# Two query tiles in one matmul of the values, eight adjoining units for them, and a longer transfer time in the plan of a four-layer kernel

## The chip, the cores and the metric

The kernel runs as one program on one core of a Trainium2 chip. The metric is the device time of one execution in microseconds (us), the median of three runs. PE is TensorE, DVE VectorE, ACT ScalarE, POOL GpSimd; SP issues most DMAs. The profile shows the TensorE clock that was granted in a stretch as a share of its full speed: 1.0 is 2.4 GHz, 0.5 is 1.2 GHz, and what lies between is a mean over time at both.

## The reference

1024 rows of 1024 float32 columns go through two blocks of two layers each. Cut to what matters here:

```
# block 1, two layers: chunked delta rule + gated linear attention
o = concat(delta_heads(x @ w_in), gla_heads(x @ w_in))
x = layer_norm(ALPHA * x + o @ w_out)
# block 2, layer 0: neighbourhood attention, layer 1: grouped attention
h = x * (1 + sc1) + sh1
y = mixer(h) @ w_o
x = layer_norm_2(ALPHA_2 * x + (1 + g1) * y)
y = hierarchical_moe(x * (1 + sc2) + sh2)      # 32 experts, top 2 of one group
x = layer_norm_2(ALPHA_2 * x + (1 + g2) * y)
# grouped attention: 16 query heads, 4 key/value heads of 64 columns
s = einsum('bqkgd,bskd->bkgqs', qb, k) * scale
p = softmax(s)
o = einsum('bkgqs,bskd->bqkgd', p, v)
```

## The kernel before

**Units.** All large data lies in 47 units ("slot", one of 128 x 1024 float32 each) that the class `Arena` hands out; a `User` has a reserve (`peak`) that others of lower rank leave free. PSUM has 8 banks. A unit can be taken as F32 or as F32R, the rounded form that PE reads in one pass. A float32 operand that must be exact is split into a high and a low F32R part (`split`: ACT rounds, DVE subtracts).

**Order.** The program is a set of generators (`Chain`) with a rank each. `Flow` gives every operation a cost and keeps a clock for each engine; the chain that may go on next emits its instructions. The costs decide nothing on the chip but the order in which instructions stand on each engine. A transfer that POOL issues is counted as `late` by the third argument of `spend`: 12 us with a `compute_op`, else 3 us. `Rows.put` adds a finished tile of 128 rows to a buffer in memory by such a transfer, and its unit is given back when the plan says that it has landed:

```
h = yield from K.A.take(user)
F.vector.tensor_mul(h.f, x.f, r.f)
F.gpsimd.dma_start(dst[t * 128:(t + 1) * 128, :], h.f, accum_op=ALU.add)
yield from F.until(F.last(h.f))
K.A.give(h)
```

**Output projections.** `out_proj_ln` runs at the end of each of the four layers' mixers, over 8 tiles of 128 rows. `load` brings a tile of the mixer's output (`oTm` in block 2) and its row of `x` (`xb`), `split` makes a high and a low part, `one` multiplies (48 matmuls of 512 columns a tile), `finish` normalises, turns the tile (8 transposes) for the next layer and calls `put`. `wout` holds 16 F32R units, the turned rows of the next layer another 16, and the mixer's late heads 4. Ahead of the first `put` `Rows.prepare` loads four rows (`ln_g`, `ln_b`, two of `mod`), computes with them, and `preset` writes the start values of the buffers, eight transfers of 512 KB each (to `xb` and to `Y`). In block 2 the last tile is followed by the routing (`route`), after which the experts start; their weights go through SP's queue too (22 units may wait), and stream without a break from then on.

**Grouped attention.** `gqa_tile` makes one tile of 128 queries of one head: 4 matmuls for the scores, maximum, exponential, scale, 8 transposes. `gqa_close` multiplies the turned probabilities of two heads with the values (`Vb`), the two heads in the two halves of PE's columns. `feed`, the projection of the next heads, fills in at a lower rank.

## Time and profile before

| | |
|---|---|
| median of 3 runs | 4102.42 us (4100.18 to 4103.45) |
| profiled execution | 4100.02 us, span 4098.2 us |
| mean granted clock | 0.967 |
| PE busy | 3826.4 us, 93% |
| DVE, ACT, POOL busy | 77%, 54%, 18% |

Nearly all instructions are recorded by one helper and so have the line L72; they are told apart by tile names and shapes. Times in a timeline count from the span's start. The layers lie, in us: hybrid 0 to 612, its projection to 745, hybrid 1 to 1284, its projection to 1435, neighbourhood attention to 1860, projection and routing to 2005, experts to 2605, layer norm to 2650, grouped attention to 3246, projection and routing to 3440, experts to 4047.

### The profile page before, as it was taken

The page shows a single profiled execution, that of the slowest core. Times are in us where ns is not written, and L with a number is a line of the kernel's source. Part 1 is how long each engine was busy: PE and PEld are TensorE (multiplying, and loading weights), DVE is VectorE, ACT ScalarE, POOL GpSimd, SP SyncE. Part 2 cuts the span into 40 slices and gives each one's busy share as a digit, 9 for nine tenths or more (in the row PEclk, how much of TensorE's full clock was granted, in tenths as well). Part 3 has the DMA queues.
Part 4 walks back from the last instruction along what each step waited for, and adds up shares of the span by engine and source line. Part 5 has one row for each costly group of instructions (what it writes and reads, how often), then busy time and mean ns, then how long its engine had stood idle before and what let it go on. Part 6 is the DMA issues. An engine that isn't in the chain of part 4 may idle for free. (4 is left out here: it accounts for less than half of the span.)

```text
span 4098.2 us, 62930 instructions
## 1 busy us (share of the span) xinstructions
PE 3826.4 (93%) x23000; PEld 3123.1 (76%) x23000; DVE 3145.8 (77%) x5986; ACT 2207.1 (54%) x3931; POOL 756.7 (18%) x608
## 2 busy tenths in 40 slices
PE   7999998999999999999799999789999987999996
PEld 6888787788888777777677777687777875777774
DVE  7777775776775687867888899866658766888887
ACT  4333343433333455442477777567778615777773
POOL 2111100211210222321222222320000011222212
PEclk9999999999999999999899999899999997999998
DMA  4223424211123544327899999610001476999993
GB/s 154 75 85 102 146 87 101 48 38 47 50 78 111 130 139 129 114 98 231 280 366 365 368 369 379 173 23 22 22 6 65 146 200 256 359 360 368 366 363 136
DMA packets 347117, 712.56 MB, mean 174 GB/s; under 512 B 60884, under 2 KB 191630, under 8 KB 346804
## 3 DMA queue, kind: packets, MB, share of 16 engines
q1 hardware_dynamic: 320308, 645.99, 44.0%
q0 software_dynamic: 26496, 62.51, 7.4%
q8 instruction: 182, 2.98, 0.3%
q14 instruction: 131, 1.07, 0.1%
HBM read 626.94 MB, written 115.44 MB: 181 GB/s over the span
## 5 line engine op out<-in xcount | busy, mean ns | idle before, releaser
L72 PE MATMUL banks<-slot 128*128 128x512 f32 (+9 forms) x18258 | 3231.3, 343 | 81.9 <-ACT slot L72 55.6
L72 PEld LDWEIGHTS banks<-slot 128*128 128x128 f32 (+5 forms) x18258 | 2547.4, 177 | 625.7 <-issue 96.9
L72 DVE TENSOR_TENSOR slot<-slot 128x1024 fp32r<-128x1024 f32 (+13 forms) x1445 | 1360.0, 964 | 245.1 <-ACT slot L72 168.2
L72 ACT ACTIVATE slot<-slot 128x1024 fp32r<-128x1024 f32 (+5 forms) x1011 | 998.1, 1016 | 630.0 <-DVE slot L72 193.3
L72 ACT ACTIVATE slot<-banks 128x512 f32<-128x512 f32 (+8 forms) x1124 | 552.4, 513 | 673.5 <-PE banks L72 611.1
L72 PE MATMUL banks<-c,slot 128*128 128x128 f32 (+2 forms) x3484 | 510.3, 283 | 93.7 <-DVE slot L72 24.0
L72 PEld LDWEIGHTS banks<-c,slot 128*128 128x128 f32 (+1 forms) x3484 | 426.3, 158 | 195.8 <-issue 53.1
L72 DVE TENSOR_TENSOR slot<-banks,slot 128x512 fp32r<-128x512 f32 (+4 forms) x622 | 360.6, 608 | 91.7 <-ACT slot L72 48.3
L72 POOL TENSOR_TENSOR slot<-slot 128x384 f32<-128x384 f32 (+2 forms) x184 | 225.6, 1251 | 982.3 <-PE banks L72 416.8
L72 ACT ACTIVATE slot<-slot,small 128x1024 f32<-128x1024 f32 (+1 forms) x292 | 266.4, 926 | 184.5 <-DVE small L72 168.1
L72 DVE COPY slot<-banks 128x512 f32<-128x512 f32 (+6 forms) x406 | 220.0, 551 | 101.6 <-PE banks L72 81.1
L72 POOL DMA_INDIRECT Y<-slot,small x62 | 146.0, 2354 | 354.7 <-DVE slot L72 232.4
L72 ACT ACTIVATE slot<-banks,small 128x1024 f32<-128x1024 f32 x140 | 156.9, 1124 | 66.4 <-DVE small L72 65.9
L72 DVE TENSOR_REDUCE small<-banks 128x1 f32<-128x1024 f32 x128 | 154.7, 1221 | 41.7 <-PE banks L72 40.1
L72 PE MATMUL banks<-slot,small 128*128 128x512 f32 (+2 forms) x388 | 156.1, 524 | 23.3 <-ACT small L72 15.0
L72 POOL MEMSET slot<- 128x1024 f32 (+1 forms) x70 | 67.6, 968 | 578.2 <-PE banks L72 371.1
L72 POOL DMA_DIRECT2D xb<-slot x40 | 35.1, 885 | 725.2 <-DVE slot L72 581.3
L72 DVE SCALAR_TENSOR_TENSOR slot<-slot,c_act 128x1024 f32<-128x1024 f32 x84 | 119.7, 1426 | 34.5 <-DMA slot<-in_ada_w 26.2
L72 DVE SCALAR_TENSOR_TENSOR small<-small 128x1 f32<-128x1 f32 (+3 forms) x590 | 120.1, 211 | 11.7
L72 DVE TENSOR_TENSOR slot<-slot,banks 128x512 f32<-128x512 f32 (+4 forms) x110 | 72.7, 666 | 72.5 <-PE banks L72 72.4
L72 PE MATMUL banks<-small,slot 128*128 128x128 f32 (+1 forms) x576 | 105.2, 297 | 21.0 <-DVE small L72 17.6
L72 ACT ACTIVATE small<-banks 128x64 f32<-128x64 f32 (+2 forms) x289 | 78.7, 273 | 76.9 <-PE banks L72 69.6
(131 smaller groups left out, 1811.6 us busy)
## 6 DMA issues: line engine op xcount, KB each, us to landing
slot<-in_moe_w_up SPq DMA_DIRECT2D x260, 512.0 KB
slot<-in_moe_w_gate SPq DMA_DIRECT2D x260, 512.0 KB
slot<-in_moe_w_down SPq DMA_DIRECT2D x260, 512.0 KB
slot<-in_ada_w SPq DMA_DIRECT2D x96, 512.0 KB
slot<-in_w_in SPq DMA_DIRECT2D x56, 512.0 KB
xb<-slot SPq DMA_DIRECT2D x40, 512.0 KB
xb<-slot POOLq DMA_DIRECT2D x40, 512.0 KB, 5.6
slot<-xb SPq DMA_DIRECT2D x24, 512.0 KB
```

The source lines that it names most:

```text
L72: r = real(*a, **k)
```

## The change

Four edits. An accumulating transfer (`accum_op`) is now counted as 12 us late in the plan. Eight of the 47 units become one tile (`wide`) of adjoining units; only F32 takes go there, and they go there first; F32R takes, and users marked `narrow`, have the other 39. In grouped attention a run is two pairs of adjoining units, and one closing multiplies two query tiles of two heads with 256 columns a matmul instead of 128. The reserves follow (`peak` 9 to 1, and 39 to 31).

```diff
-            self._flow.spend(self._name, self._cost(op, a, k), outs, ins, (12.0 if "compute_op" in k else 3.0) if "dma" in op else 0.0)
+            self._flow.spend(self._name, self._cost(op, a, k), outs, ins, (12.0 if "compute_op" in k or "accum_op" in k else 3.0) if "dma" in op else 0.0)
...
+        if n == 1:
+            t = {i: (i >= self.wide, t) for i, t in self.free.items() if not narrow or i >= self.wide}
+            i = min(t, key=lambda i: (t[i], i), default=None)
+            return None if i is None else (self.free[i], i)
+        for i in range(0, self.wide - n + 1, min(n, 4)):
...
+        narrow = dt != F32 or (user is not None and user.narrow)
+
+        def fits():
+            found = self.find(n, narrow)
+            if found is None or self.wide < self.n and found[1] < self.wide:
+                return found is not None
+            return sum(i >= self.wide or self.wide == self.n for i in self.free) - n >= self.kept(user)
...
+N_WIDE = 8
...
+    wide = arena.tile([128, N_WIDE * 1024], F32, name="wide")
+
+    def unit(i, n, dt):
+        if i >= N_WIDE:
+            return arena.tile([128, 1024], dt, name="slot", tag=f"slot{i}")
+        return wide[:, i * 1024:(i + n) * 1024]
...
         for i in range(2):
-            T.matmul(p.f[64 * i:64 * i + 64, 0:128], v, PT[i].rows()[:, kc], start=(kc == 0), stop=(kc == NT - 1))
-        if kc % 4 == 3:
+            T.matmul(p.f[64 * i:64 * i + 64, 0:256], v, PT[i].f.rearrange("p (q c j) -> p q c j", q=2, j=128)[:, :, kc],
+                     start=(kc == 0), stop=(kc == NT - 1))
+        if kc % 2:
             yield
...
-    F.vector.tensor_copy(oS.f[:, q * 128:(q + 1) * 128], p.f[:, :128])
+    F.vector.tensor_copy(oS.f[:, q * 128:(q + 2) * 128], p.f[:, :256])
...
+    base.narrow = fd.narrow = K.W.user.narrow = True
...
-    att.peak = 9
+    att.peak = 1
...
-    for _ in range(4):
-        runs.append((0.0, (yield from several(A, 2, att))))
+    for _ in range(2):
+        runs.append((0.0, [(yield from A.take(att, n=2)), (yield from A.take(att, n=2))]))
...
-            for q in range(NT):
+            for q in range(0, NT, 2):
...
-    user.peak = 39
+    user.peak = 39 - N_WIDE
```

The cost and the units change the plan, and so the order of instructions everywhere. Three places follow; the rows give the matmul's output and inputs by tile names, columns, and how many stand in a row.

PE at the first output projection, before: the matmuls of 512 columns are `one`'s (and at the end the next layer's), the eights and sixteens of `c` with 128 columns are `finish`'s transposes.

```order
L72 MATMUL banks<-c_68,slot 128x128 x8
L72 MATMUL banks<-slot 128x512 x78
L72 MATMUL banks<-c_68,slot 128x128 x8
L72 MATMUL banks<-slot 128x512 x48
L72 MATMUL banks<-c_68,slot 128x128 x8
L72 MATMUL banks<-slot 128x512 x210
L72 MATMUL banks<-c_68,slot 128x128 x16
L72 MATMUL banks<-slot 128x512 x30
L72 MATMUL banks<-c_68,slot 128x128 x16
L72 MATMUL banks<-slot 128x512 x42
L72 MATMUL banks<-c_68,slot 128x128 x16
```

The same place now:

```order
L72 MATMUL banks<-c_69,wide 128x128 x8
L72 MATMUL banks<-slot 128x512 x29
L72 MATMUL banks<-c_69,wide 128x128 x8
L72 MATMUL banks<-slot 128x512 x44
L72 MATMUL banks<-c_69,wide 128x128 x8
L72 MATMUL banks<-slot 128x512 x42
L72 MATMUL banks<-c_69,wide 128x128 x8
L72 MATMUL banks<-slot 128x512 x50
L72 MATMUL banks<-c_69,wide 128x128 x8
L72 MATMUL banks<-slot 128x512 x49
L72 MATMUL banks<-c_69,wide 128x128 x8
L72 MATMUL banks<-slot 128x512 x48
```

The transposes of tiles 2 to 7 stood in pairs behind 210 matmuls; now each tile's eight stand some 42 to 50 matmuls behind the last.

SP at the third output projection, before, from the third tile's loads on (`oTm` and `xb` are loads, `xb` and `Y` on the left are presets):

```order
L185 DMA slot<-oTm_11371 128x7x128
L185 DMA slot<-xb_85 128x1024
L185 DMA slot<-oTm_11371 128x7x128 x2
L185 DMA slot<-xb_85 128x1024
L185 DMA slot<-mod_80 128x1024
L185 DMA slot<-oTm_11371 128x7x128
L185 DMA slot<-xb_85 128x1024
L185 DMA xb_86<-slot 128x1024 x8
L185 DMA slot<-in_ln_b 128x1024
L185 DMA Y_15128<-slot 128x1024 x8
L185 DMA slot<-in_moe_w_up 128x1024
L185 DMA slot<-in_moe_w_gate 128x1024
```

The same queue now, from the first tile's load on:

```order
L185 DMA slot<-xb_86 128x1024
L185 DMA wide<-in_moe_w_up 128x1024
L185 DMA wide<-in_moe_w_gate 128x1024 x2
L185 DMA xb_87<-slot 128x1024 x8
L185 DMA slot<-in_ln_b 128x1024
L185 DMA slot<-in_moe_w_up 128x1024 x2
L185 DMA wide<-in_moe_w_gate 128x1024 x2
L185 DMA slot<-in_moe_w_up 128x1024
L185 DMA Y_14739<-slot 128x1024 x8
L185 DMA slot<-oTm_11150 128x7x128
L185 DMA slot<-xb_86 128x1024
L185 DMA slot<-oTm_11150 128x7x128
```

Before, the loads of the first tiles stood ahead of both presets. Now the first tile's load is the only one ahead of them (its first row stands four rows above the first that is shown), and eight expert weights stand between and ahead of the presets too.

PE in grouped attention in its steady stretch, before (128x512 are scores, `c` 128x128 transposes, 64x128 the closing):

```order
L72 MATMUL banks<-c_68,slot 128x128 x3
L72 MATMUL banks<-slot 64x128
L72 MATMUL banks<-c_68,slot 128x128 x8
L72 MATMUL banks<-slot 128x512 x6
L72 MATMUL banks<-slot 64x128 x5
L72 MATMUL banks<-c_68,slot 128x128 x8
L72 MATMUL banks<-slot 64x128 x2
L72 MATMUL banks<-slot 128x512 x2
L72 MATMUL banks<-slot 64x128 x9
L72 MATMUL banks<-slot 128x512 x8
L72 MATMUL banks<-c_68,slot 128x128 x12
L72 MATMUL banks<-slot 64x128 x16
```

And now (64x256 the closing):

```order
L72 MATMUL banks<-wide,slot 64x256 x11
L72 MATMUL banks<-slot 128x512 x4
L72 MATMUL banks<-c_69,wide 128x128 x16
L72 MATMUL banks<-slot 128x512 x10
L72 MATMUL banks<-c_69,wide 128x128 x12
L72 MATMUL banks<-c_69,slot 128x128 x8
L72 MATMUL banks<-wide,slot 64x256
L72 MATMUL banks<-c_69,wide 128x128 x4
L72 MATMUL banks<-wide,slot 64x256 x7
L72 MATMUL banks<-c_69,wide 128x128 x4
L72 MATMUL banks<-wide,slot 64x256 x5
L72 MATMUL banks<-slot 128x512 x2
```

The pieces of scores and transposes have become longer, and a closing of 256 columns takes the place of two of 128.

## Rows read from the trace of the kernel before

**Rows 1.** The page, its first part: busy time, share of the span, instructions.

```profile
PE 3826.4 (93%) x23000; PEld 3123.1 (76%) x23000; DVE 3145.8 (77%) x5986; ACT 2207.1 (54%) x3931; POOL 756.7 (18%) x608
```

**Rows 2.** Windows by stage: width, busy (count) by engine, clock, DMA share, GB/s.

```profile
60.00:612.00 552.00, 526.06 (x3690) 448.00 (x3689) 427.90 (x918) 195.03 (x442) 91.52 (x52) 0.97 0.32 95
612.00:745.00 133.00, 118.03 (x534) 94.76 (x533) 85.61 (x254) 61.80 (x141) 9.09 (x10) 0.94 0.42 98
745.00:1284.00 539.00, 520.88 (x3706) 445.17 (x3706) 378.54 (x883) 196.56 (x446) 91.17 (x52) 0.98 0.19 58
1284.00:1435.00 151.00, 138.51 (x631) 113.22 (x630) 102.59 (x272) 63.76 (x151) 25.28 (x28) 0.94 0.47 125
...
1860.00:2005.00 145.00, 123.64 (x710) 103.06 (x710) 102.14 (x314) 28.93 (x40) 21.06 (x23) 0.92 0.80 228
...
2605.00:2650.00 45.00, 30.02 (x118) 21.24 (x117) 43.88 (x131) 27.41 (x68) 22.70 (x39) 0.77 0.59 127
...
2735.00:3246.00 511.00, 484.44 (x4231) 394.36 (x4230) 356.59 (x646) 416.10 (x776) 21.66 (x28) 0.98 0.11 35
3246.00:3440.00 194.00, 154.74 (x790) 129.05 (x786) 120.52 (x339) 42.99 (x52) 26.29 (x27) 0.85 0.68 201
```

**Rows 3.** Timeline of PE at the first output projection: start, duration, group, [idle before].

```profile
702.41 4.34 PE L72 MATMUL banks<-slot 128*128 128x512 f32 x18
718.44 1.22 PE L72 MATMUL banks<-slot 128*128 128x512 f32 x2 [11.69 <-ACT slot L72]
```

**Rows 4.** Timeline of ACT at the same place.

```profile
710.45 1.06 ACT L72 ACTIVATE slot<-slot 128x1024 fp32r<-128x1024 f32 x1 [7.64 <-DMA slot<-in_w_in]
```

**Rows 5.** Windows after the two stalls, columns as in the second group.

```profile
718.40:732.00 13.60, 10.79 (x41) 8.12 (x41) 12.09 (x41) 8.04 (x16) 1.73 (x2) 0.75 0.25 39
...
1391.00:1405.00 14.00, 13.88 (x56) 10.69 (x57) 12.34 (x33) 8.84 (x15) 2.87 (x3) 0.80 0.70 174
```

**Rows 6.** Timeline of PE at the second output projection.

```profile
1376.72 4.34 PE L72 MATMUL banks<-slot 128*128 128x512 f32 x18
1390.97 8.51 PE L72 MATMUL banks<-slot 128*128 128x512 f32 x23 [9.91 <-ACT slot L72]
```

**Rows 7.** Timeline of ACT at the same place, and its split there.

```profile
1384.48 1.06 ACT L72 ACTIVATE slot<-slot 128x1024 fp32r<-128x1024 f32 x1 [5.66 <-DMA slot<-in_na_w_qkv]
```

**Rows 8.** Timeline of POOL at the end of the neighbourhood attention.

```profile
1855.45 1.92 POOL L72 TENSOR_TENSOR slot<-slot,small 128x384 f32<-128x384 f32 x2 [4.51 <-PE banks L72]
```

**Rows 9.** Timeline of SP's DMA issues at the third output projection.

```profile
1880.64 7.83 SPq L185 DMA_DIRECT2D xb<-slot  x8
...
1897.30 9.12 SPq L185 DMA_DIRECT2D Y<-slot  x8
```

**Rows 10.** Timeline of PE at the third output projection.

```profile
1868.86 13.56 PE L72 MATMUL banks<-slot 128*128 128x512 f32 x66
1882.26 1.03 PE L72 MATMUL banks<-c,slot 128*128 128x128 f32 x8
```

**Rows 11.** Windows at the third output projection.

```profile
1896.00:1974.00 78.00, 77.89 (x431) 65.75 (x429) 54.38 (x163) 12.66 (x16) 10.49 (x12) 1.00 0.91 251
```

**Rows 12.** Groups by form of PE and its weight loads, 2735 to 3246.

```profile
L72 PE MATMUL banks<-slot 128*64 128x128 f32 x2048 | 145.9, 279 | 8.7 <-DVE slot L72 5.4 <-ACT slot L72 3.3
...
L72 PEld LDWEIGHTS banks<-slot 128*64 128x64 f32 x2048 | 114.1, 136 | 37.7 <-issue 22.3 <-DVE slot L72 7.2 <-ACT slot L72 5.7
```

**Rows 13.** Timeline of PE in grouped attention, a closing and a half unbroken.

```profile
2870.84 2.84 PE L72 MATMUL banks<-slot 128*64 128x128 f32 x48
```

**Rows 14.** Timeline of PE in grouped attention, half a closing alone.

```profile
3138.96 1.09 PE L72 MATMUL banks<-slot 128*64 128x128 f32 x16
```

**Rows 15.** Windows in grouped attention.

```profile
3100.00:3200.00 100.00, 99.25 (x895) 78.13 (x894) 82.75 (x143) 91.22 (x135) 0.00 (x0) 1.00 0.10 33
```

**Rows 16.** Timeline of PE at the fourth output projection.

```profile
3309.38 2.93 PE L72 MATMUL banks<-slot 128*128 128x36 f32 x10 [5.20 <-ACT slot L72]
```

**Rows 17.** Timeline of ACT at the fourth output projection.

```profile
3307.89 0.95 ACT L72 ACTIVATE slot<-slot 128x896 fp32r<-128x896 f32 x1 [11.74 <-DMA slot<-oTm]
```

More of the change, by code (lines that the diff above doesn't have):

```diff
@@ L277, in __init__ @@
     def __init__(self, order, peak):
-        self.order, self.peak, self.held = order, peak, 0
+        self.order, self.peak, self.held, self.narrow = order, peak, 0, False
 class Arena:
-    def __init__(self, flow, n, make, fresh=False):
+    def __init__(self, flow, n, make, fresh=False, wide=None):
         self.flow, self.n, self.make, self.fresh = flow, n, make, fresh
+        self.wide = n if wide is None else wide
         self.free = {i: 0.0 for i in range(n)}
@@ L295, in leave, with find @@
         self.users.remove(u)
-    def find(self, n):
+    def find(self, n, narrow=False):
         best = None
         if n == 1:
-            return min(((t, i) for i, t in self.free.items()), default=None)
-        for i in range(0, self.n - n + 1, min(n, 4)):
+            t = {i: (i >= self.wide, t) for i, t in self.free.items() if not narrow or i >= self.wide}
+            i = min(t, key=lambda i: (t[i], i), default=None)
+            return None if i is None else (self.free[i], i)
+        for i in range(0, self.wide - n + 1, min(n, 4)):
             if all(i + j in self.free for j in range(n)):
@@ L311, in take @@
     def take(self, user=None, n=1, dt=F32):
-        fits = lambda: len(self.free) - n >= self.kept(user) and self.find(n) is not None
+        narrow = dt != F32 or (user is not None and user.narrow)
[4 more added lines that the diff above has]
+            return sum(i >= self.wide or self.wide == self.n for i in self.free) - n >= self.kept(user)
         while not fits():
@@ L317, in now @@
     def now(self, n=1, dt=F32, user=None):
-        t, i = self.find(n)
+        t, i = self.find(n, dt != F32 or (user is not None and user.narrow))
         for j in range(n):
@@ L398, in setup @@
     K.F = F = Flow(tc)
-    K.A = Arena(F, N_SLOTS, lambda i, n, dt: arena.tile([128, 1024], dt, name="slot", tag=f"slot{i}"), fresh=True)
+    wide = arena.tile([128, N_WIDE * 1024], F32, name="wide")
[3 more added lines that the diff above has]
+        return wide[:, i * 1024:(i + n) * 1024]
+    K.A = Arena(F, N_SLOTS, unit, fresh=True, wide=N_WIDE)
     small = arena.tile([128, N_SMALL * 32], F32, name="small")
@@ L2170, in gqa_close @@
         for i in range(2):
-            T.matmul(p.f[64 * i:64 * i + 64, 0:128], v, PT[i].rows()[:, kc], start=(kc == 0), stop=(kc == NT - 1))
-        if kc % 4 == 3:
+            T.matmul(p.f[64 * i:64 * i + 64, 0:256], v, PT[i].f.rearrange("p (q c j) -> p q c j", q=2, j=128)[:, :, kc],
+                     start=(kc == 0), stop=(kc == NT - 1))
+        if kc % 2:
             yield
     runs.append((F.cur.time, PT))
-    F.vector.tensor_copy(oS.f[:, q * 128:(q + 1) * 128], p.f[:, :128])
+    F.vector.tensor_copy(oS.f[:, q * 128:(q + 2) * 128], p.f[:, :256])
     K.banks.give(p)
-    oS.left -= 1
+    oS.left -= 2
     if not oS.left:
@@ L2259, in gqa_mixer @@
     yield k_ready
-    att.peak = 9
+    att.peak = 1
     runs = []
-    for _ in range(4):
-        runs.append((0.0, (yield from several(A, 2, att))))
+    for _ in range(2):
+        runs.append((0.0, [(yield from A.take(att, n=2)), (yield from A.take(att, n=2))]))
+    K.W.user.narrow = False
     own = [b for _, r in runs for b in r]
@@ L2282, in gqa_mixer @@
                 tiles = []
-                for i in range(2):
-                    while len(open_) >= 8:
-                        yield open_.pop(0)
-                    e = F.spawn(gqa_tile(K, Q[i], KH[c], KL[c], q * 128, PT[i].f), prio + 2 + 0.01 * n)
-                    n += 1
-                    tiles.append(e)
-                    open_.append(e)
+                for j in range(2):
+                    for i in range(2):
+                        while len(open_) >= 8:
+                            yield open_.pop(0)
+                        P = PT[i].f[:, j * 1024:(j + 1) * 1024]
+                        e = F.spawn(gqa_tile(K, Q[i], KH[c], KL[c], (q + j) * 128, P), prio + 2 + 0.01 * n)
+                        n += 1
+                        tiles.append(e)
+                        open_.append(e)
                 closed.append(F.spawn(gqa_close(K, tiles, PT, runs, Vb, c, oS, q, outs[2 * c + pr], Q), prio + 4))
@@ L2895, in moe_layer @@
     if N is not None:
-        yield from N.X.take()
+        yield from N.X.take(N.X.user)
     def close():
@@ L2946, in main @@
             K.A.leave(N.X.user)
+            N.X.user.narrow = True
             after = Rows(xb[4], g, b)
```

## The prediction

> **What bounds the kernel now.** I read the page's busy shares first: TensorE (PE) is busy 93% of the span [rows 1], so the time is PE's work plus the gaps that PE stands in. The table by stage then says where those gaps are [rows 2]: 15.0 us (133.0 − 118.03) in the stretch around the first output projection, 12.5 around the second, 21.4 around the third with the routing behind it, 15.0 in the layer norm from 2605 to 2650, 26.6 in grouped attention and 39.3 around the fourth projection. The bodies of the two hybrid layers hold another 25.9 and 18.1 us in over 500 us each. The half clock sits in the same places: the granted clock is 0.77 in 2605 to 2650 and 0.85 in 3246 to 3440, against 0.97 or more where PE runs without a break [rows 2]. So the change is worth what it does to about five gaps and to the order inside grouped attention; the stream of expert weights between them is left with the same operations.
>
> Each large gap has a named cause. At the first projection PE stands 11.69 us before 718.44, released by ACT [rows 3]; ACT itself had waited 7.64 us until 710.45 for a load of the next layer's `w_in` [rows 4]: as I read the code, the unit that the load goes to was still held by an accumulating transfer of a finished tile. After the stall the clock is 0.75 for 13.6 us [rows 5]. At the second projection it is the same shape, 9.91 us [rows 6] behind ACT's 5.66 us wait for `na_w_qkv` [rows 7], and a clock of 0.80 over 14 us [rows 5]. At the fourth, PE stands 5.20 us for ACT [rows 16], which waited 11.74 us for a load of `oTm` [rows 17].
>
> **The change, part by part.** The plan is made with costs, so a cost that is changed moves the order everywhere; I price the places where a gap stands.
>
> *First projection.* The planner now believes that a unit under an accumulating transfer comes back 9 us later. The first order excerpt shows what follows: `finish` of tiles 2 to 7 no longer stands in pairs at the end but after each tile's matmuls, and the late split of `w_in` comes after them. That can take away at most the 15.0 idle us of this stretch [rows 2] and the half clock behind the stall, (1 − 0.75) × 13.6 = 3.4 us [rows 5]: 18.4. Against it stands that F32R units come from 39 instead of 47: 16 hold `wout`, 16 the turned rows of the next layer and 4 the late heads, so that only one tile's hi/lo pair can be made ahead. A split row in ACT takes 1.06 us [rows 4] and the subtraction on DVE beside it about as long; if each of 8 tiles stands for one such row, 8.5 us go back. I take −8 us, between −18.4 and +1.
>
> *Second projection.* The same edit: at most 9.91 + (1 − 0.80) × 14 = 12.7 us back [rows 5, 6], the same 8.5 us against it. I take −4 (−12.7 to +5).
>
> *Third projection.* This is where I expect a loss. The second excerpt shows SP's queue. Before, the loads of `oTm` and `xb` for tiles 1 to 6 stood ahead of the presets (eight `xb`, one `ln_b`, eight `Y`, 512 KB each). Now three expert weights, the eight `xb` presets, `ln_b`, five more weights and the eight `Y` presets stand between tile 0 and tile 1. SP issues in order, so tile 1 waits for all of them. The first weights wait for POOL's last additions of the neighbourhood attention, which end at 1855.45 + 1.92 = 1857.4 [rows 8]. From the first preset to the last it took 1880.64 to 1906.42, 25.8 us [rows 9]. A transfer costs 9.12 / 8 = 1.14 us there [rows 9]; the eight weights add up to 8 × 1.14 = 9.1, of which the five behind `ln_b` may lie in the 8.8 us between the last `xb` and the first `Y` [rows 9]. So tile 1's load goes out between 1857.4 + 25.8 = 1883.2 and 1892.3, and with two transfers of 1.14 us to land and ACT's split of 0.95 [rows 17] tile 1 starts between 1886 and 1895. Before, tile 0's matmuls were over at about 1874.3: of the 66 matmuls up to 1882.3 at 0.205 us each [rows 10], the last 39 were tile 1's by the order. PE is busy 77.89 of the 78 us from 1896 to 1974 [rows 11], so that what is lost here is lost at the end: 1886 − 1874.3 to 1895 − 1874.3, less tile 0's end that is now done earlier (eight transposes, 1.03 us [rows 10], and eight small matmuls of 0.29 [rows 16]): 8 to 17 us. Then a half clock as after the first stall, 3.4 us, and DVE's routing, which the new order weaves into the last two tiles, 0 to 8 us. I take 13 + 3 + 2 = +18 (8 to 29).
>
> *Layer norm into grouped attention.* The new order lets some of the K and V projection of grouped attention start inside the 15.0 us that PE idles from 2605 to 2650 [rows 2]. What is done there is missing later: −4 (−8 to 0).
>
> *Values.* 2048 records of 128 columns [rows 12] become 1024 of 256 columns. Half a closing standing alone (16 records) takes 1.09 us [rows 14], 48 in a row take 2.84 [rows 13]: 2.18 against 1.89 for the 32 records of a closing. If all that the longer matmuls give is the better of the two, 64 closings × 0.29 = 18 us would be the top; but the next piece starts before the last has ended, so most of the 0.29 lies beside other work. −4 (−18 to 0). The copies on DVE (64 of 128 columns become 32 of 256) are off PE's path.
>
> *Grouped attention's order.* The third excerpt: four tiles of scores, then their transposes, then one closing, where it used to be two and half as much. From 3100 to 3200 PE is busy 99.25% and ACT 91.22% [rows 15]: nothing to gain there, and ACT can lose only 9% before it bounds. Elsewhere the 26.6 idle us [rows 2] can go either way. I take 0 (−10 to +10).
>
> *Fourth projection.* Four pairs of `oTm` and `xb` loads now stand ahead of the presets, where the stall of 5.20 us was a wait for `oTm` [rows 16, 17]. −4 (−5 to +8).
>
> *Hybrid bodies.* Same work, another weave, and 44 idle us in them [rows 2]. 0 (−10 to +10).
>
> **A rule against the sum.** In the trace a record of the values takes 59 ns in an unbroken piece (2.84 / 48) [rows 13], with weight loads of 64 columns that are busy 114.1 us beside 145.9 of matmul [rows 12]. The Trainium skill (TensorE: Matmul & The Clock Gate, section Back-to-back issue gap) says that in a stream of weight load and matmul pairs both set the spacing, and gives about 81 ns at 128 columns against 56 for the matmul by itself. By that rule, as an estimate, 2048 × 81 = 166 us would shrink to 1024 matmuls of 256 columns at its table's 262 cycles, 112 us, and the kernel would end 54 us sooner. The trace doesn't bear it out: 59 ns lie by the matmul's own figure.
>
> **Sum.** −8 − 4 + 18 − 4 − 4 + 0 − 4 + 0 = −6 us. The profiled execution took 4100.02 us (span 4098.2 and 1.8 around it), the median of the three runs is 4102.42. −6 on the median is 4096.4; I say 4096.
>
> **The rivals.** A difference of about 0.2% (8 us: below 4094 or above 4110.6) is the least that a measurement tells from none.
> - *The two early stalls go whole, and the queue at the third is covered* (faster): −18.4 − 12.7 − 4 − 4 − 4 + 8 = −35, 4067 us. For it: the finishes are spread evenly in the order. Against: the shortage of F32R units, and presets that nothing shortens.
> - *SP's queue at its full price* (slower): 29 at the third projection, and at the other two the F32R shortage eats the gain to −2 together: 29 − 2 − 4 − 4 − 4 = +15, 4117 us. It decides from about 22 us of delay at the third on, if the rest stays at −14. For it: PE has work without a break behind that point [rows 11], and nothing else to fill in.
> - *Coarser runs starve PE in grouped attention* (slower): if ACT loses 1 us at each of the 32 closings, +32 − 6, 4128 us. For it: ACT at 91%. Against: eight tiles may still be open, and the feed fills gaps in the first half.
> - *Weight loads were not hidden*: if half of the 114.1 us [rows 12] had been bare, −57, 4045 us. Against it: PE's other work in the stretch, 484.4 − 145.9 = 338.5 us, leaves 172 of its 511 [rows 2], too little for 145.9 and 114.1 end to end [rows 12]. The Trainium skill's rule named above is of this kind.
> - *The change does nothing*: the places cancel by chance or PE's work alone counts, 4102 us.
>
> **How the numbers follow.** The trade (gains at two projections, loss at the third) 0.38, with its own range 4084 to 4108: 0.13 of it faster, 0.22 the same, 0.03 slower. Whole gain 0.24; full queue 0.20; starved attention 0.10; bare weight loads 0.03; nothing 0.05 (the same). Faster 0.13 + 0.24 + 0.03 = 0.40; the same 0.27; slower 0.33. The range reaches into both neighbours: 4066 (the whole gain's time, less 1 us) to 4126, leaving out the weight loads, most of the starved case and the ends.
>
> **What would show it.** Right: no PE gap above 3 us at 707 to 745 and 1380 to 1405; a PE gap of 9 to 18 us after the first tile of the third projection, with `xb` and `Y` presets on SP just ahead of tile 1's `oTm`; the values' records at twice 57 to 60 ns, so that their share of PE hardly falls; PE idle in grouped attention near 27 us. Wrong: stalls in the first two projections that only moved to another wait, a third projection with no gap, or idle time in grouped attention above 40 us or below 15.

## The result and the profile after

The changed kernel takes 4169.9 us, the median of four runs (4165.77 to 4175.34), against 4102.93 (4100.18 to 4104.39) for the kernel before: a ratio of 1.0171, with an interval of 1.0158 to 1.0184. It is 67 us slower. I had forecast 4096 us, no change that a measurement can tell, in a range of 4066 to 4126. The profiled execution took 4170.96 us over a span of 4167.8.

The first part of the page, as in [rows 1]: TensorE has 1024 matmuls less, and yet it is busy 46 us longer.

```profile
PE 3872.3 (93%) x21976; PEld 3107.1 (75%) x21976; DVE 3138.7 (75%) x5954; ACT 2194.7 (53%) x3929; POOL 766.1 (18%) x608
```

The windows of the changed kernel, with the columns of [rows 2], cut where PE gives the first matmul of the next stage: hybrid 0, first projection, hybrid 1, second projection, neighbourhood attention, third projection and routing, experts, layer norm, grouped attention, fourth projection and routing, experts with the last layer norm.

```profile
0.00:614.80 614.80, 569.93 (x3874) 474.69 (x3875) 450.32 (x1020) 223.44 (x525) 92.48 (x59) 0.97 0.34 103
614.80:715.00 100.20, 96.90 (x443) 76.69 (x442) 76.84 (x215) 54.89 (x124) 8.21 (x9) 1.00 0.54 131
715.00:1297.80 582.80, 558.15 (x3792) 475.55 (x3791) 394.55 (x921) 202.20 (x460) 94.39 (x53) 0.95 0.19 54
1297.80:1400.70 102.90, 96.91 (x443) 76.68 (x441) 77.54 (x217) 46.23 (x115) 10.02 (x13) 0.99 0.52 138
1400.70:1879.80 479.10, 455.99 (x2681) 359.81 (x2682) 367.59 (x840) 228.03 (x499) 134.85 (x129) 0.97 0.38 117
1879.80:2055.60 175.80, 133.40 (x731) 111.62 (x730) 100.01 (x330) 33.72 (x55) 19.05 (x22) 0.83 0.70 205
...
2781.50:3325.90 544.40, 494.26 (x3181) 357.01 (x3181) 354.24 (x615) 413.49 (x778) 22.15 (x28) 0.97 0.08 28
3325.90:3523.30 197.40, 156.04 (x805) 128.05 (x803) 121.73 (x339) 42.80 (x54) 22.78 (x24) 0.87 0.69 209
```

The same cuts in the kernel before, for the three stages that lost most:

```profile
718.40:1284.70 566.30, 545.14 (x3799) 462.28 (x3799) 399.70 (x945) 214.39 (x482) 92.90 (x54) 0.98 0.20 58
...
1857.20:2002.60 145.40, 124.04 (x711) 102.78 (x711) 103.55 (x315) 27.81 (x39) 18.98 (x22) 0.92 0.81 229
...
2732.60:3246.10 513.50, 486.55 (x4238) 395.80 (x4238) 358.84 (x650) 418.41 (x781) 21.66 (x28) 0.98 0.11 35
```

The table has all stages: each kernel's profiled execution less that of before, in us, by these cuts. The row of the changed kernel adds up to 69.6, the difference of the two spans. The losses are in grouped attention (+31.0), the third projection (+30.4), hybrid 1 (+16.5) and the neighbourhood attention (+12.8); the last experts and the last norm gave 17.7 back. The other rows are the experiments'.

| kernel | hyb 0 | 1st proj | hyb 1 | 2nd proj | neighb. | 3rd proj | experts | norm | grouped | 4th proj | last | span |
|---|---|---|---|---|---|---|---|---|---|---|---|---|
| changed | +1.6 | −5.1 | +16.5 | −3.3 | +12.8 | +30.4 | −3.5 | −0.5 | +31.0 | +7.4 | −17.7 | 4167.8 |
| e1 | +0.9 | −3.5 | +0.5 | −5.0 | +2.6 | +19.4 | +0.2 | −0.1 | +6.2 | −1.3 | −18.2 | 4099.7 |
| e2 | 0.0 | +0.5 | +14.3 | −6.4 | +14.2 | +29.5 | −1.0 | +1.2 | +31.2 | +10.8 | −4.8 | 4187.8 |
| e3 | −3.9 | −5.5 | +23.8 | −3.3 | +11.5 | +29.3 | −4.4 | −2.1 | +4.5 | +3.0 | +10.6 | 4161.8 |
| e4 | +4.7 | −1.2 | +0.6 | −1.2 | −1.8 | −0.2 | +0.4 | −0.1 | +26.2 | −0.2 | +0.6 | 4125.9 |
| e5 | +6.2 | −5.5 | +19.6 | −4.2 | +9.4 | +32.9 | −4.7 | +1.1 | +4.5 | +2.6 | +11.3 | 4171.4 |
| e6 | −1.4 | −5.4 | +17.2 | −2.7 | +1.8 | +12.0 | −5.2 | −0.4 | +30.5 | +10.9 | −11.4 | 4144.1 |
| e7 | +1.3 | −3.8 | +4.6 | −4.8 | −9.7 | +7.0 | −4.1 | +0.7 | +9.0 | +6.3 | +1.1 | 4105.9 |
| e8 | −1.5 | −6.6 | −5.4 | +12.6 | +16.2 | +29.0 | −4.3 | +0.5 | +5.3 | −0.6 | −18.6 | 4124.9 |
| e9 | +11.0 | −4.6 | +19.2 | +12.6 | +17.1 | +29.4 | −3.7 | +1.6 | +6.4 | −0.2 | −18.8 | 4168.4 |
| e10 | +1.2 | −1.2 | +2.2 | −2.1 | −1.7 | −0.5 | −0.4 | −3.4 | +2.7 | +0.7 | −0.1 | 4095.6 |
| e11 | +0.4 | −0.2 | +3.1 | −0.4 | +0.4 | −0.5 | −1.0 | +0.9 | +12.8 | +0.4 | −2.4 | 4111.7 |
| e12 | −2.2 | −1.3 | +1.6 | −2.9 | −1.0 | −0.3 | +0.4 | −0.3 | +20.2 | +12.9 | −0.2 | 4125.2 |
| e13 | +1.2 | −3.8 | +0.2 | −5.3 | −11.9 | +7.4 | −5.0 | +0.7 | +3.6 | +2.5 | −18.3 | 4069.5 |

One execution is good to a few us in a stage: where an experiment left a stage's code alone (e4, e10, e11 up to the third projection), the stage moved by up to 4.7.

**The first projection did what was forecast.** PE's timeline at its end: the pieces of 45 to 48 matmuls follow each other without a gap, each behind the eight transposes of a finished tile. The 11.69 us of [rows 3] are gone, and PE is idle for 3.3 us in the whole projection (100.20 − 96.90, in the windows above); gaps of 3.15 and 1.81 us in the head of the next layer are left.

```profile
697.91 11.50 PE L72 MATMUL banks<-slot 128*128 128x512 f32 x48
709.35 1.09 PE L72 MATMUL banks<-c,wide 128*128 128x128 f32 x8
710.20 10.48 PE L72 MATMUL banks<-slot 128*128 128x512 f32 x45
723.99 2.07 PE L72 MATMUL banks<-w,wide 17*128 17x256 f32 x4 [3.15 <-DVE small L72]
727.87 1.97 PE L72 MATMUL banks<-c,wide 128*128 128x128 f32 x8 [1.81 <-ACT wide L72]
```

**The second projection did half of it.** The 9.91 us of [rows 6] have become 4.33, with 2.17 more at 1405.05, and ACT still waits for loads of `na_w_qkv` there:

```profile
1400.81 2.07 PE L72 MATMUL banks<-slot 128*128 128x512 f32 x4 [4.33 <-ACT slot L72]
```

**The third projection shows the queue.** POOL's last additions of the neighbourhood attention end at 1877.38 + 2.77 = 1880.15:

```profile
1877.38 2.77 POOL L72 TENSOR_TENSOR slot<-wide,small 128x384 f32<-128x384 f32 x2
```

SP's timeline, which answers to [rows 9]: both groups of presets stand ahead of tile 1's `oTm`, as the order said.

```profile
1877.45 0.33 SPq L185 DMA_DIRECT2D wide<-in_moe_w_up  x1
1879.30 1.21 SPq L185 DMA_DIRECT2D wide<-in_moe_w_gate  x2
1880.60 6.28 SPq L185 DMA_DIRECT2D xb<-slot  x8
...
1899.13 6.76 SPq L185 DMA_DIRECT2D Y<-slot  x8
1906.81 0.37 SPq L185 DMA_DIRECT2D slot<-oTm  x1
```

ACT at the same place waits for that load, and PE for ACT:

```profile
1921.99 0.95 ACT L72 ACTIVATE slot<-slot 128x896 fp32r<-128x896 f32 x1 [16.12 <-DMA slot<-oTm]
```

```profile
1902.39 1.08 PE L72 MATMUL banks<-wide,slot 128*128 128x36 f32 x8 [0.66 <-DVE slot L72]
1923.00 15.17 PE L72 MATMUL banks<-slot 128*128 128x512 f32 x54 [19.53 <-ACT slot L72]
```

The windows of the stall and of what follows it: the DMA engines are full (share 1.04, 357 GB/s) while PE stands, and the clock is 0.70 behind it.

```profile
1902.00:1918.00 16.00, 1.08 (x8) 0.97 (x8) 5.11 (x17) 1.24 (x1) 1.74 (x2) 0.57 1.04 357
1918.00:1935.00 17.00, 12.00 (x41) 9.33 (x42) 4.37 (x4) 3.80 (x4) 0.00 (x0) 0.70 0.78 262
```

So tile 1's load went out at 1906.81, and its data were split 15.2 us later, at 1921.99. I had given the two transfers 2.3 us, twice the 1.14 at which SP had issued the presets [rows 9]. That is the time from one issue to the next, not the time until the data are there: as I read these windows, a load that has left SP still stands behind the bytes of the presets and the weights that were issued before it. The Trainium skill (DMA: Bandwidth & Descriptors, section Issuing engines are not separate DMA queues) says that transfers run on the same 16 DMA engines and interleave there, whichever engine starts them; the share of 1.04, those engines full, agrees.

**Grouped attention: the records did not shrink, and the waits doubled.** The groups by form, 2781.5 to 3325.9. The values stand in the first line; the last closing's 32 records lie behind the end of this window.

```profile
L72 PE MATMUL banks<-wide,slot 128*64 128x256 f32 x992 | 147.9, 400 | 1.3 <-ACT wide L72 1.3
```

```profile
L72 PEld LDWEIGHTS banks<-wide,slot 128*64 128x64 f32 x992 | 73.5, 140 | 51.4 <-issue 19.8 <-ACT wide L72 5.4 <-DVE small L72 0.4
```

In PE's timeline an unbroken piece of them is 2.81 / 24 = 117 ns a record, twice the 59 ns of [rows 13]:

```profile
3236.00 2.81 PE L72 MATMUL banks<-wide,slot 128*64 128x256 f32 x24
```

So half as many matmuls and weight loads take the same time: 147.9 us busy for 992, 151.6 for all 1024, against 145.9 for 2048 [rows 12], although the weight loads fell from 114.1 to 73.5. The Trainium skill (TensorE: Matmul & The Clock Gate, section Back-to-back issue gap) gives about 81 ns at 128 columns for a stream of weight load and matmul pairs. The gain of 54 us that the prediction estimates from it, and doubts, did not come: the runs side with the rows. What PE waits for in this stage (us in total, times, longest), in the kernel before, then in the changed one:

```profile
PE banks L72 <- ACT slot L72: 16.8, 31, 2.0
```

```profile
PE banks L72 <- ACT wide L72: 39.7, 54, 2.1
```

### The profile page after: what moved, and what is told of

It is laid out like the page before. It is cut to its first block, busy times and chain, and to the rows that moved or that the text cites. A ratio compares the mean times of both kernels' runs of the same rounds, so it can differ in the third digit from the quotient of the medians.

```text
span 4167.8 us, 60590 instructions
## 1 busy us (share of the span) xinstructions
PE 3872.3 (93%) x21976; PEld 3107.1 (75%) x21976; DVE 3138.7 (75%) x5954; ACT 2194.7 (53%) x3929; POOL 766.1 (18%) x608
## 5 line engine op out<-in xcount | busy, mean ns | idle before, releaser
L72 PE MATMUL banks<-slot 128*128 128x512 f32 (+6 forms) x14626 | 2979.7, 361 | 86.1 <-ACT slot L72 40.1
L72 PEld LDWEIGHTS banks<-slot 128*128 128x128 f32 (+4 forms) x14626 | 2329.6, 186 | 581.3 <-ACT slot L72 65.5
L72 DVE TENSOR_TENSOR slot<-slot 128x1024 fp32r<-128x1024 f32 (+13 forms) x924 | 822.8, 910 | 119.9 <-ACT slot L72 72.2
L72 ACT ACTIVATE slot<-slot 128x1024 fp32r<-128x1024 f32 (+5 forms) x602 | 604.3, 1029 | 392.1 <-PE banks L72 123.7
L72 ACT ACTIVATE slot<-banks 128x512 fp32r<-128x512 f32 (+10 forms) x822 | 400.4, 513 | 508.4 <-PE banks L72 473.4
L72 ACT ACTIVATE slot<-wide 128x1024 fp32r<-128x1024 f32 (+4 forms) x358 | 358.1, 1018 | 214.3 <-PE banks L72 75.1
L72 DVE TENSOR_TENSOR slot<-wide,slot 128x1024 fp32r<-128x1024 f32 (+6 forms) x366 | 420.8, 1164 | 49.9 <-ACT slot L72 42.1
L72 PE MATMUL banks<-c,wide 128*128 128x128 f32 (+3 forms) x1828 | 269.1, 282 | 61.4 <-ACT wide L72 29.4
L72 PE MATMUL banks<-c,slot 128*128 128x128 f32 (+1 forms) x1656 | 250.2, 288 | 57.3 <-issue 17.7
L72 PEld LDWEIGHTS banks<-c,slot 128*128 128x128 f32 x1656 | 213.1, 169 | 100.4 <-issue 35.2
L72 PEld LDWEIGHTS banks<-wide,slot 128*64 128x64 f32 (+1 forms) x1216 | 102.7, 150 | 57.5 <-issue 20.2
```

What stands on the lines that cost most here:

```text
L72: r = real(*a, **k)
```

## The experiments

Three theories stood at the start. The queue: presets ahead of tile 1 cost the end of the neighbourhood attention and the third projection. The runs: four tiles to a closing starve PE in grouped attention. The units: 39 F32R units, or the rule that F32 goes to the eight, make the plan of the hybrid layers worse. Their rivals: the longer cost in the plan does it all; the 256-column matmul itself is slow; the one large tile makes instructions wait for each other that have nothing to do with each other. Totals stand beside the kernel before as it ran with them: 4109.62 us beside e1 to e4 (one run), 4097.33 beside e5 to e7 (13 runs), 4096.08 beside e8 to e10 (one run), 4097.65 beside e11 to e13 (11 runs, 4085.63 to 4123.61). Of the experiments only e7 and e13 have more than one run of their own, so a difference of some 20 us between totals says little in the others; their stages are read instead.

**e1, the cost alone.** The kernel before with the first line of the diff.

```diff
-  (12.0 if "compute_op" in k else 3.0) if "dma" in op else 0.0)
+  (12.0 if "compute_op" in k or "accum_op" in k else 3.0) if "dma" in op else 0.0)
```

> Kernel before with one line changed: accumulating transfers count 12 us late in the plan. Theory A (the loss comes from the runs of four tiles in grouped attention, about +31, from the SP queue at the third projection, about +30, and from the eight units set apart, about +30 in hybrid 1 and the neighbourhood layer): here grouped attention stays within 5 us of its 513, hybrid 1 and the neighbourhood layer stay within 5 us of before, the first two projections gain 3 to 8 us each, and since this kernel too has the presets ahead of tile 1's load on SP, the third projection loses 15 to 30 us; total 4100 to 4125. Rival B (the later time in the plan makes the order worse everywhere, the units are harmless): hybrid 1 +16 and neighbourhood +13 show here as well; total 4140 or more.

Measured: 4101.6 us against 4109.62 (one run each). SP's queue has the presets ahead of tile 1 here too:

```profile
1848.66 7.81 SPq L185 DMA_DIRECT2D xb<-slot  x8
...
1868.35 7.64 SPq L185 DMA_DIRECT2D Y<-slot  x8
1876.09 1.11 SPq L185 DMA_DIRECT2D slot<-oTm  x1
```

The cost by itself gains at both early projections (−3.5, −5.0) and in the last layer (−18.2), and loses 22.0 us at the third (+2.6 and +19.4). It leaves hybrid 1 alone and is not the cause of the 67 us.

**e2, the change without the cost.** The same line undone in the changed kernel.

```diff
-  (12.0 if "compute_op" in k or "accum_op" in k else 3.0) if "dma" in op else 0.0)
+  (12.0 if "compute_op" in k else 3.0) if "dma" in op else 0.0)
```

> Changed kernel with accumulating transfers back at 3 us in the plan: the units and the pairs alone. Theory A: grouped attention still about +31, third projection about +30 (its SP queue has the same rows), hybrid 1 and neighbourhood layer together +20 to +30; total 4160 to 4185. Rival B: the losses outside grouped attention go, total 4125 to 4140.

Measured: 4189.6 us, a little above the range expected. Hybrid 1, the neighbourhood attention, the third projection and grouped attention lose as in the changed kernel, so the units and the runs are enough for these losses. At the third projection the cost alone is enough too (e1): with either edit SP has the presets ahead of tile 1. At the first projection the gain is gone (+0.5), so that one was the cost's.

**e3, adjoining units without pairs.** The changed kernel with four runs of two adjoining units (`Half` is one of the two) and the old closing of 128 columns.

```diff
-            T.matmul(p.f[64 * i:64 * i + 64, 0:256], v, PT[i].f.rearrange("p (q c j) -> p q c j", q=2, j=128)[:, :, kc],
-                     start=(kc == 0), stop=(kc == NT - 1))
+            T.matmul(p.f[64 * i:64 * i + 64, 0:128], v, PT[i].rows()[:, kc], start=(kc == 0), stop=(kc == NT - 1))
...
-    for _ in range(2):
-        runs.append((0.0, [(yield from A.take(att, n=2)), (yield from A.take(att, n=2))]))
+    for _ in range(4):
+        w = yield from A.take(att, n=2)
+        own.append(w)
+        runs.append((0.0, [Half(w, 0), Half(w, 1)]))
```

> Changed kernel with grouped attention as before: one query tile a closing, 128 columns a matmul, four runs of two units (which are adjoining units here); units set apart and the 12 us stay. Theory A (coarse runs starve PE): grouped attention falls from 544 to 510 to 520 us, everything ahead of it as in the changed kernel; total 4130 to 4145. Rival C (the narrow users, 39 units for the projections that feed it, cost grouped attention its time): it stays at 535 to 550; total 4160 to 4175.

Measured: 4163.63 us, where 4130 to 4145 had been expected. Grouped attention is back at +4.5 (517.9 us), as the theory had it; the rest of the loss stays, in hybrid 1 (+23.8) and around the third projection. What the total missed stands in the last layer: +10.6, where the changed kernel has −17.7. No theory had that, and its cause is open.

**e4, coarse runs alone.** The kernel before, separate units, 128 columns, but two runs of four tiles and one closing for four.

```diff
-    for _ in range(4):
-        runs.append((0.0, (yield from several(A, 2, att))))
+    for _ in range(2):
+        runs.append((0.0, (yield from several(A, 4, att))))
...
-            for q in range(NT):
+            for q in range(0, NT, 2):
```

> Kernel before with grouped attention in two runs of four tiles (two query tiles of two heads closed together, still matmuls of 128 columns, from any units), nothing else changed. Theory A: grouped attention takes 535 to 550 us instead of 513, the rest within 5 us of before; total 4125 to 4140. Rival C: grouped attention stays within 8 us of 513, total 4095 to 4110.

Measured: 4127.64 us, grouped attention +26.2, no other stage beyond 4.7. PE's waits there are those of the changed kernel:

```profile
PE banks L72 <- ACT slot L72: 37.2, 57, 2.2
```

From e3 to the changed kernel grouped attention grows by 31.0 − 4.5 = 26.5. Coarse runs alone give 26.2, so the coarse runs are the loss, and the 256-column matmul, on which the edit turns, gave and cost nothing that these executions can tell.

**e5, the rules without the large tile.** e3 with eight separate tiles in place of `wide`, the rules on who may take them kept; grouped attention waits until all eight are free before it takes its runs.

```diff
-    wide = arena.tile([128, N_WIDE * 1024], F32, name="wide")
...
-    K.A = Arena(F, N_SLOTS, unit, fresh=True, wide=N_WIDE)
+    K.A = Arena(F, N_SLOTS, lambda i, n, dt: arena.tile([128, 1024], dt, name="slot", tag=f"slot{i}"), fresh=True, wide=N_WIDE)
```

> As e3 (grouped attention with one query tile a closing), but the eight units are eight tiles of their own again, under the same rules: only F32 takes, F32 first, 39 for F32R. Theory A (the rules make the plan worse: F32R takes find fewer units): hybrid 1 stays 10 us or more above before, the neighbourhood layer 8 or more, the third projection about +30; total 4140 to 4175. Rival D (one tile ties instructions together that share nothing, so the waits come from the tile): hybrid 1 and the neighbourhood layer come back to within 5 us of before; total 4110 to 4130.

Measured: 4173.56 us (before on this chip 4097.33, 4088.92 to 4106.98 in 13 runs); hybrid 1 +19.6, third projection +32.9. The theory of the one tile falls: the losses stay without it.

**e6, the changed kernel with late presets.** The start values are made only once tile 3's load is on its way, in block 2.

```diff
-    F.spawn(after.prepare(K, user), prio - 0.45)
+    if freed is None:
+        F.spawn(after.prepare(K, user), prio - 0.45)
...
             ins.append(e)
+            if t == 3 and freed is not None:
+                F.spawn(after.prepare(K, user), prio - 0.45)
```

> Changed kernel, with one edit in the output projections of the second block: the row loads and presets are asked for only when the load of the fourth tile begins, so that they can't stand ahead of tiles 1 and 2 on SP. Theory A (the 30 us of the third projection are SP's queue): it takes 145 to 155 us instead of 176, total 4140 to 4150. Rival E (39 units for F32R are the cause, tile 1's split waits anyway): it stays at 168 or more, total 4160 to 4180.

Measured: 4145.9 us. The neighbourhood attention goes from +12.8 to +1.8 and the third projection from +30.4 to +12.0: 29.4 of the 43.2 us come back, so these are the price of presets that stand early. At the third projection the way is SP's queue, as shown above. The neighbourhood attention ends at 1879.8 in the changed kernel, ahead of the first preset's issue at 1880.60, so its 11.0 us come by another way than SP's queue, and no run shows which. 157.4 us for the third stage is more than the 145 to 155 expected; what the other 12.0 come from isn't shown.

**e7, the cost with late presets.** e1 with the same edit one tile earlier, at both projections of block 2.

```diff
+            if t == 2 and freed is not None:
+                F.spawn(after.prepare(K, user), prio - 0.45)
```

> Kernel before with the 12 us for accumulating transfers and late presets (asked for when the load of the third tile begins). The 12 us alone lost 19 us at the third projection to the queue and won 8 at the first two and 19 in the last layer. Theory A: with the queue in order the third projection is back to 145 to 152 us and the total is 4075 to 4090, faster than both kernels. Rival E: the third projection keeps 160 or more and the total is 4095 to 4105.

Measured: 4101.18 us (4088.49 to 4108.09, 10 runs), a ratio of 1.0007 (0.9993 to 1.0022): a miss. The neighbourhood attention and the third projection are as hoped: −9.7 and +7.0 against e1's +2.6 and +19.4, or −2.7 against +22.0 together, which is the better figure, since the cut between the two stages, PE's first matmul of the projection, moves with the order. But the fourth loses (+6.3, e1 −1.3) and the 18.2 us of the last layer are gone (+1.1). These stages are those of the slowest of the ten executions; e13, which leaves the fourth projection's presets early, bears them out.

**e8 and e9, how many units F32R may have.** e5 with the same first choice of units and no `narrow` users; F32R may take 43 units (e8) or all 47 (e9).

```diff
-            t = {i: (i >= self.wide, t) for i, t in self.free.items() if not narrow or i >= self.wide}
+            t = {i: ((i < self.wide) if narrow else (i >= self.wide), t) for i, t in self.free.items() if not narrow or self.wide == self.n or i >= self.wide - 4}
...
-    base.narrow = fd.narrow = K.W.user.narrow = True
```

In e9 the condition behind `self.free.items()` is left out as well. From grouped attention on, both have the old rules and the old closing.

> Eight separate units under the new rules up to grouped attention (F32 first in the eight, 12 us in the plan), but F32R may take 43 of the 47 units, the four extra ones last; from grouped attention on the old rules and the old closing. Theory A1 (what hybrid 1 lost, +17 to +24, comes from too few units for F32R): hybrid 1 is between before's 566 and 575, the third projection still has its queue (165 to 178); total 4105 to 4130. Rival A2 (it comes from F32 going first to the same eight units, so that each of them is waited for): hybrid 1 stays at 578 or more.

> As e8, but F32R may take all 47 units, the eight last. Theory A1: hybrid 1 within 5 us of before's 566. Rival A2: 578 or more. Grouped attention within 8 us of 513 in either.

Measured: 4126.85 and 4170.66 us (before 4096.08, one run). Hybrid 1 is −5.4 with 43 units and +19.2 with 47, where 39 gave +19.6 (e5): no rule in the number. The two losses are not alike, though. In e9 PE is idle for 585.5 − 548.9 = 36.6 us of hybrid 1 and its work grew by 3.8; in e5 it is idle for 23.4 and its work grew by 17.3. So whether 39 units are too few for hybrid 1, my reason against the early projections, stays open. Both kernels also lose 12.6 us at the second projection, where PE waits 18.2 us (e8) and 17.7 us (e9) for ACT in one piece.

**e10, three runs of two tiles.** The kernel before with six units in place of eight for the probabilities.

```diff
-    for _ in range(4):
+    for _ in range(3):
```

> Kernel before with three runs of two tiles in grouped attention instead of four (six units in flight instead of eight), nothing else. Theory F (what the coarse runs cost, +26, is that only four tiles can be under way while four are closed, where four fine runs leave six): three fine runs leave four under way as well, so grouped attention takes 530 to 545 us. Rival G (the cost lies in the longer pieces of one kind on PE, not in the tiles under way): it stays within 8 us of 513.

Measured: 4097.64 us, grouped attention +2.7. A smaller ring of runs isn't what starves PE. PE's waits for ACT grew here too, to 28.6 us in 45 times, and the stage hardly did: the wait table by itself gives no price.

**e11 and e12, which part of the coarse run costs.** Both start from e4. In e11 each query tile is closed as soon as its own two tiles are done, and the four units come back together; in e12 the closing waits for all four, and each pair of units comes back by itself.

```diff
-    for e in tiles:
-        yield e
...
     for j in range(2):
+        for e in tiles[2 * j:2 * j + 2]:
+            yield e
+        yield
+        p = yield from K.banks.take()
```

> As e4 (two runs of four tiles, 128 columns), but each query tile is closed as soon as its own two tiles are done; the four units still come back together. Theory H1 (the coarse runs cost 26 us because no closing may start before all four tiles are done): grouped attention is back to 513 to 522 us. Rival H2 (because units come back four at a time, so that new tiles start in lumps): it stays at 532 or more.

```diff
-    runs.append((F.cur.time, PT))
...
+        runs.append((F.cur.time, PT[2 * j:2 * j + 2]))
...
-    for _ in range(2):
-        runs.append((0.0, (yield from several(A, 4, att))))
+    for _ in range(4):
+        runs.append((0.0, (yield from several(A, 2, att))))
```

> As e4, but the two units of a query tile come back when that tile is closed; the closings still wait for all four tiles, and four tiles are started together, when two pairs are free. Theory H1: grouped attention stays at 532 or more. Rival H2: back to 513 to 522.

Measured: 4113.76 and 4127.14 us; grouped attention +12.8 and +20.2 (526.2 and 533.7 us), PE's wait for ACT 27.8 and 35.7 us. Without the wait for all four tiles 13.4 of the 26.2 come back, about half; without the return of the units in one piece 6.0, and e12 loses 12.9 at the fourth projection in their place. e12 lies where H1 had it, e11 between the ranges of H1 and H2, so neither theory holds alone. How the rest divides is open.

**e13, the cost with late presets at the third projection alone.**

```diff
+    held = freed is not None and prio < 400
+    if not held:
+        F.spawn(after.prepare(K, user), prio - 0.45)
...
+            if t == 2 and held:
+                F.spawn(after.prepare(K, user), prio - 0.45)
```

> Kernel before with the 12 us for accumulating transfers, and late presets (asked for at the load of the third tile) in the third projection alone. In its SP queue seven of the eight oTm loads stand ahead of the presets. Theory A (the late queue was the only loss of the 12 us alone): the third projection takes 145 to 152 us, the first two projections keep their -8 and the last layer its -19; total 4072 to 4090, ratio to before 0.993 to 0.998. Rival (each change of the plan moves other places by chance by as much): total 4092 to 4110, ratio 0.998 to 1.002.

Measured: 4068.04 us (4060.27 to 4074.61, 6 runs) against 4097.65: a ratio of 0.9921 (0.9896 to 0.9946), faster than both kernels and a little better than either theory had it. The neighbourhood attention and the third projection together are at −4.5, where the cost alone has +22.0. Of the 28.7 us that the profiled execution gained, 18.3 stand in the last layer, for which there is no explanation. SP has seven loads of `oTm` ahead of the presets now, and the eighth stands between their two groups:

```profile
1856.81 0.36 SPq L185 DMA_DIRECT2D slot<-oTm  x1
...
1873.71 7.62 SPq L185 DMA_DIRECT2D xb<-slot  x8
1881.37 1.18 SPq L185 DMA_DIRECT2D slot<-in_ln_b  x1
1889.09 0.37 SPq L185 DMA_DIRECT2D slot<-oTm  x1
1890.57 6.54 SPq L185 DMA_DIRECT2D Y<-slot  x8
```

PE's next tile follows without a stall: in its timeline 100 matmuls stand in a row.

```profile
1877.95 1.03 PE L72 MATMUL banks<-c,slot 128*128 128x128 f32 x8
1878.74 21.43 PE L72 MATMUL banks<-slot 128*128 128x512 f32 x100
```

## Why the prediction was wrong

*Grouped attention's order, "0 (−10 to +10)", is the step that failed most:* +31.0, of which 26 are the coarse runs (e4, and e3 against the changed kernel). I read one stretch in which PE is busy 99.25% [rows 15] and took the stage to have nothing to lose but ACT's last 9%. The rival was there, at +32 − 6 and a chance of 0.10; its price was right within 6 us, by luck: the 1 us that ACT was to lose at each closing came from no row. Against it I had set that eight tiles may still be open and that the feed fills gaps. That did not save it: PE's waits for ACT went from 31 to 54, with a longest of 2.0 and 2.1 us, and e11 and e12 show part of what brings them. I had named idle time above 40 us as the mark of a wrong forecast; it is 544.40 − 494.26 = 50.1 us.

*Third projection, "+18 (8 to 29)":* the mechanism is right in each link, SP's queue, tile 1, ACT's split, PE. The size is +30.4, and PE's gap 19.53 us where 9 to 18 was to be the sign. The mis-sized term is the landing: 2.3 us taken, 15.2 measured, because I had read the spacing of SP's issues as the time of a transfer. Ahead of it the sum was sound: tile 1's load went out 26.7 us after POOL's last additions, where 25.8 to 34.9 had been worked out. The 12.8 us of the neighbourhood attention ahead of it I had not priced at all; 11.0 of them come back when the presets are late (e6).

*Hybrid bodies, "0 (−10 to +10)":* +18.1, 16.5 of it in hybrid 1, and this came from no step: "same work, another weave" was taken at nothing. Idle time there grew from 21.2 to 24.6 us only; PE's own work took 13 us longer, at a clock of 0.95 for 0.98. PE waits longer for DVE's small tiles, in the kernel before and then in the changed one:

```profile
PE banks L72 <- DVE small L72: 6.1, 6, 2.4
```

```profile
PE banks L72 <- DVE small L72: 18.5, 9, 3.5
```

Over the kernels that wait goes with the loss: 14.4 to 18.5 us in the changed kernel, e2, e3, e5, e6 and e9, which lose 14.3 to 23.8, and 6.1 to 8.2 us in all others, which lose at most 4.6. (In e9 waits for ACT's and for DVE's units, 14.4 us each, weigh as much.) The windows behind one such wait of 2.44 us show where the time goes: PE is busy 99% of the second and still at 0.65.

```profile
935.00:955.00 20.00, 16.76 (x81) 14.69 (x82) 12.65 (x23) 3.45 (x12) 1.93 (x1) 0.67 0.11 28
955.00:975.00 20.00, 19.89 (x117) 18.22 (x116) 8.40 (x16) 3.93 (x9) 1.49 (x1) 0.65 0.10 26
```

Why the plans with the new rules for units bring these waits is open: the one tile doesn't explain them (e5), the number of units for F32R shows no rule (e8, e9), and e8 has most of the rules without the loss in hybrid 1. I have no run that holds the order and changes the wait alone.

*Values, "−4 (−18 to 0)":* 0, the near end (26.5 with the longer matmul, 26.2 without it). The records doubled in length, as the rows had it, and their gaps were covered before.

*First and second projection, "−8" and "−4":* −5.1 and −3.3, right in sign. At the first the mechanism is right too, and e1 and e2 show it as the cost's own; a gap of 3.15 us just behind it is barely over the 3 that I had allowed. At the second a gap of 4.33 us is left, the kind of stall that I had thought gone; there either edit alone gives 5 to 6, and they don't add up.

*Layer norm, "−4":* −0.5 up to grouped attention's start; that its early projections shorten the stage behind can't be seen under the +31. *Fourth projection, "−4 (−5 to +8)":* +7.4, near the far end. The changed kernel, e2 and e6, which have the units and the runs, lose 7.4 to 10.9 there; with the units alone it is +3.0 and +2.6 (e3, e5), with the runs alone −0.2 (e4). e12 loses 12.9 without the units, so the cause is open. The last layer's −17.7 was in no step. e1 has −18.2, but e3, e5 and e7 hold the same cost and lose there, so it hangs on the plan as a whole.

The sum counted five gaps and let the long stages stand still. They moved by 62 us (hybrid 0 and 1, neighbourhood and grouped attention), and the gaps by 29.

## What to carry to other kernels

A shorter or longer instruction is worth little where the next one starts before it has ended; look at how much must be finished before the next piece may start, since runs of four tiles with one closing, instead of two, cost 26 us here, about half of it for the wait for all four, and the matmul that they were made for gave nothing. Where an in-order queue holds large writes ahead of a small load, count the load's landing behind their bytes, not from its issue, and try to move the writes behind the loads: with that at the third projection, the one useful line of this change made the kernel 0.8% faster (e13), though most of that stands in the last layer, where I can't explain it. A planner's costs and supplies move every stage, so each part of such a change is worth running alone.

## What had not been expected of the hardware

DVE's additions of 128 x 512 from units to units take 0.68 us in hybrid 1, and 1.5 to 2.4 us each while POOL does a `TENSOR_TENSOR` of 128 x 1024. DVE's timeline in the changed kernel, then POOL's:

```profile
926.16 0.67 DVE L72 TENSOR_TENSOR slot<-wide 128x512 f32<-128x512 f32 x1
927.58 2.98 DVE L72 TENSOR_TENSOR slot<-wide 128x512 f32<-128x512 f32 x2
930.74 2.12 DVE L72 TENSOR_TENSOR slot<-wide 128x512 f32<-128x512 f32 x1
933.18 1.99 DVE L72 TENSOR_TENSOR slot<-slot 128x512 f32<-128x512 f32 x1
935.09 2.38 DVE L72 TENSOR_TENSOR slot<-wide,slot 128x512 f32<-128x512 f32 x1
937.40 0.68 DVE L72 TENSOR_TENSOR slot<-slot 128x512 f32<-128x512 f32 x1
```

```profile
927.60 2.42 POOL L72 TENSOR_TENSOR slot<-c,g 128x1024 fp32r<-128x1024 f32 x1 [5.51 <-PE banks L72]
929.98 4.64 POOL L72 TENSOR_TENSOR slot<-c,small 128x1024 f32<-128x1024 f32 x2
934.58 2.34 POOL L72 TENSOR_TENSOR slot<-c,g 128x1024 fp32r<-128x1024 f32 x1
```

The five slow ones take 9.47 us where 5 × 0.68 = 3.4 would do, and PE's wait of 2.44 us stands behind them:

```profile
939.23 0.49 PE L72 MATMUL banks<-small,slot 128*128 128x128 f32 x2 [2.44 <-DVE small L72]
```

The Trainium skill (SBUF — State Buffer, section Who interferes with whom) says that a DVE instruction with two inputs in SBUF and a GpSimd instruction that reads SBUF exclude each other, since they share a port; these rows agree. It is in the kernel before as well, where three such additions from 932.03 take 4.90 us beside POOL's at 934.04, so it is no cause of the difference by itself.
